# Narrow rows for a second group of modulation weights, softmax scaling on another engine, and a new order of work and loads

## The chip, the cores and the metric

The kernel runs on one core of a Trainium2 chip. The metric is the device time of one execution in microseconds (us), lower is better; the number given for a kernel is the median of its timed runs. The core has five engines that run their own instruction queues in order and wait for each other by semaphores: TensorE (PE; its weight loads are listed apart as PEld), VectorE (DVE), ScalarE (ACT), GpSimd (POOL) and SyncE (SP), which here issues all loads.

## What is computed

Two blocks in float32, batch 1, 256 tokens of width 1024, with a second stream of 256 context tokens in the first of the first block's two layers.

```python
def first_block(x, c, ctx, c_ctx, w_mod, b_mod, ...):
    xl, xc = x, ctx
    for i in range(DEPTH):                      # 2 layers
        ml = (jax.nn.silu(c) @ w_mod[i] + b_mod[i]).reshape(B, N_MOD, 1, D)
        mc = (jax.nn.silu(c_ctx) @ w_mod[i] + b_mod[i]).reshape(N_MOD, D)
        hl = modulate(xl, ml[:, 0], ml[:, 1])
        hc = modulate(xc, mc[0], mc[1])
        if i % 2 == 0:                          # latent attention and pooling windows
            oc, ol = mla_pool_mixer(hc, hl, mix0_w_in[j], ...)
        else:                                   # grouped-query attention
            oc, ol = gqa_mixer(hc, hl, gqa_w_in[j], ...)
        xl = xl + ml[:, 2] * ol
        xl = xl + ml[:, 5] * conv_ffn(modulate(xl, ml[:, 3], ml[:, 4]), ...)
        if not last:
            ...                                 # the same for xc
    return rms_norm(xl, g_final)
```

`modulate(x, shift, scale)` is `rms_norm(x) * (1 + scale) + shift`. The second block is an FFN, a mixer of differential and dilated attention with gates, and another FFN.

## The kernel before, in words

Each weight and activation is split into a high and a low part (`whi`, `wlo`) of the type fp32r, and a product is three matmuls (`mm3`) or two (`mm2`). A weight comes by DMA into one of three `raw` tiles, ACT copies the high part out of it and DVE subtracts it for the low part (`parts`).

Nothing is issued in the order in which the code is written. `Program.record` collects every operation with its dependencies, and `Program.schedule` places them on the five engines by a list schedule: it prices each operation (`price`), adds latencies between engines, gives out tiles from pools (`SLOTS`), and of what is ready takes the one with the lowest index, moved by `shift`. The order in which operations start in this plan is the order on each engine's queue. So a new price or a new rule of the planner moves instructions on every engine.

The parts that matter here, in order of time:

- `setup` loads `cc` (the two conditioning vectors, padded to 32 columns), one stream's X, `ident`, `vecs` and the first pair of `wm` tiles, and issues 100 filler matmuls (`warm`) whose result is not used.
- `mod_chunk(k)` computes shift and scale of layer 0's first normalisation for one of eight blocks of 128 columns. Its 16 matmuls have `sc`, 32 columns wide, as weights, so each uses 32 columns of the array, and four of them stand beside each other. I call a matmul of that shape a narrow row.
- `layer0_mixer` takes the sums of squares (`norm`), and for each of eight k-blocks computes h (`modulated`) and accumulates `p` (pooling input), `cq` of the first stream; then `ckv` of the first stream, transposes (`cT`), the same two products for the second stream, the pooling windows on POOL and DVE (tiles `pp`, `df`, `d`, product `po`), `uk`, `uv`, `uq`, and attention over eight heads (`qkT`, scores `s`, softmax in `e`, transposes `pt`, output `o`).
- `mod_group(g)` computes the other modulation vectors, six groups with eight `raw` tiles each. For a group in `WHOLE` (before: group 0) PE multiplies each tile with four narrow rows. For the others DVE accumulates `raw` times a column of `sc` in `macc`, and PE sums the result over partitions at the end. Group 1 is computed beside `uk` to `uq`, group 0 beside the attention, and groups 2 to 5 beside the FFN of layer 0.
- `softmax_t` has the row maximum on DVE, exp on ACT, the reciprocal on DVE and the scaling (`times`) on DVE for the wide rows of layer 0 (512), on ACT for its narrow ones (256) and for layer 1 (512).

## Time and profile before

| | us |
|---|---|
| three timed runs | 1569.17, 1565.89, 1565.12 |
| their median | 1565.89 |
| the profiled execution | 1562.85 |
| its span, first to last instruction | 1561.1 |
| PE busy | 1534.3 (98%) |
| DVE busy | 1147.6 (74%) |
| ACT busy | 829.1 (53%) |
| POOL busy | 100.1 (6%) |

The share of the longest engine says what bounds the kernel as a whole, but it is an average over stages, and a matmul that is counted as busy may be filler. The rows further down therefore come from stretches of the span. In rows of a timeline the first two numbers are the start in us from the beginning of the span and the busy time of the group of instructions; `xN` is their number, and what stands in brackets is the engine's idle time just before and what ended it. A matmul with fp32 operands (a narrow row, for one) leaves two records; a transpose, or a matmul with fp32r operands, leaves one.

### The profile page before, as it was taken

To read this page: it belongs to the slowest core of one execution; us is meant where nothing else is said; L and a number is where in the kernel's file an instruction comes from. 1 tells how busy PE (TensorE), PEld (TensorE's weight loads), DVE (VectorE), ACT (ScalarE), POOL (GpSimd) and SP (SyncE) were. 2 spreads that over 40 slices of the span, in tenths; PEclk is the share of its full clock that TensorE was granted. 3 is DMA by queue.
4 is the path that set the end of the run, shared out by engine and by line. 5 is a ranking of instruction groups with operands and counts; after the bars stand their busy time and mean duration, and the time that the engine had idled before them with its cause. 6 is when DMAs were issued, how large, how long until landed. Compare 5 with 4: busy or idle time off the path is not lost.

```text
span 1561.1 us, 23690 instructions
## 1 busy us (share of the span) xinstructions
PE 1534.3 (98%) x9226; PEld 1340.2 (86%) x9226; DVE 1147.6 (74%) x2117; ACT 829.1 (53%) x1532; POOL 100.1 (6%) x116
## 2 busy tenths in 40 slices
PE   9989999999999999999999999999999999999998
PEld 7877798888788888999888888888999999888886
DVE  5598889648964856889987787765887786687752
ACT  5356844231331334686876675554765565475550
POOL 0040000000000000110000011100000000111100
PEclk9999999999999999999999999999999999999999
DMA  9345353334753642222665564455423345454450
GB/s 373 117 133 215 135 177 133 123 109 180 257 185 133 245 155 86 84 107 109 237 221 192 177 227 162 163 206 197 166 87 114 122 168 200 173 216 162 162 189 27
DMA packets 41375, 258.47 MB, mean 166 GB/s; under 512 B 4784, under 2 KB 5168, under 8 KB 15664
## 3 DMA queue, kind: packets, MB, share of 16 engines
q1 hardware_dynamic: 41264, 256.97, 45.9%
q8 instruction: 72, 1.18, 0.3%
q14 instruction: 39, 0.32, 0.1%
HBM read 255.90 MB, written 1.05 MB: 165 GB/s over the span
## 4 chain that ended last, share of the span: by engine, by line
PE 88%; DVE 4%; ACT 1%; issue 1%; POOL 1%; DMA 0%; DVEq 0%; POOLq 0%; ACTq 0%; SPq 0%
PE g L401 18%; PE u L401 18%; PE dn L401 12%; PE tm L401 10%; PE y L401 8%; PE out L401 4%; PE gate L401 3%; PE s L401 3%; PE o L401 3%; PE pt L401 2%; PE pa L401 1%; PE mod L401 1%; PE uq L401 1%; DVE wlo L401 1%; DVE h L401 1%
## 5 line engine op out<-in xcount | busy, mean ns | idle before, releaser
L401 DVE TENSOR_TENSOR wlo<-raw,whi 128x1024 fp32r<-128x1024 f32 (+4 forms) x393 | 460.3, 1185 | 81.7 <-PE y L401 26.8
L401 ACT ACTIVATE whi<-raw 128x1024 fp32r<-128x1024 f32 (+4 forms) x393 | 394.1, 1025 | 221.5 <-PE dn L401 59.8
L401 PE MATMUL dn<-mid,whi 128*128 128x512 f32 (+1 forms) x576 | 172.2, 373 | 0.0
L401 PE MATMUL g<-h,whi 128*128 128x512 f32 (+1 forms) x528 | 169.7, 388 | 0.9 <-ACT h L401 0.8
L401 PE MATMUL u<-h,whi 128*128 128x512 f32 (+1 forms) x528 | 167.9, 385 | 0.0
L401 PE MATMUL tm<-whi,a 128*128 128x256 f32 (+1 forms) x576 | 126.8, 306 | 0.1
L401 PEld LDWEIGHTS dn<-mid,whi 128*128 128x128 f32 x576 | 105.0, 188 | 20.4 <-issue 0.8
L401 PE MATMUL dn<-mid,wlo 128*128 128x256 f32 (+1 forms) x376 | 121.6, 323 | 0.0
L401 PE MATMUL g<-a,whi 128*128 128x512 f32 x336 | 118.9, 392 | 0.0
L401 PE MATMUL u<-a,whi 128*128 128x512 f32 x336 | 118.7, 392 | 0.0
L401 PEld LDWEIGHTS g<-h,whi 128*128 128x128 f32 x528 | 99.2, 190 | 22.6 <-ACT h L401 0.9
L401 PEld LDWEIGHTS u<-h,whi 128*128 128x128 f32 x528 | 98.8, 188 | 19.8
L401 PE MATMUL g<-h,wlo 128*128 128x256 f32 (+1 forms) x344 | 115.0, 335 | 0.4 <-DVE wlo L401 0.4
L401 PE MATMUL u<-h,wlo 128*128 128x256 f32 (+1 forms) x344 | 114.6, 333 | 0.0
L401 PE MATMUL y<-whi,mid 128*128 128x512 f32 x352 | 109.0, 389 | 0.0
L401 DVE SCALAR_TENSOR_TENSOR macc<-raw,sc,macc 128x1024 f32<-128x1024 f32 x84 | 107.0, 1298 | 2.6 <-DMA raw<-wmod 2.4
L401 PEld LDWEIGHTS tm<-whi,a 128*128 128x128 f32 x576 | 95.2, 190 | 1.4 <-DVE a L401 0.3
L401 PE MATMUL g<-a,wlo 128*128 128x256 f32 x336 | 94.2, 280 | 0.0
L401 PE MATMUL u<-a,wlo 128*128 128x256 f32 x336 | 94.1, 280 | 0.0
L401 POOL TENSOR_TENSOR small<-small,mhalf 128x2 f32<-128x2 f32 (+2 forms) x34 | 34.2, 1007 | 895.1 <-DVE small L401 725.3
L401 PE MATMUL tm<-wlo,a 128*128 128x256 f32 (+1 forms) x288 | 87.6, 305 | 0.0
L401 PEld LDWEIGHTS y<-whi,mid 128*128 128x128 f32 x352 | 66.1, 188 | 13.7
(342 smaller groups left out, 3205.4 us busy)
## 6 DMA issues: line engine op xcount, KB each, us to landing
raw<-wup SPq DMA_DIRECT2D x44, 1024.0 KB, 4.8
raw<-wgu SPq DMA_DIRECT2D x44, 1024.0 KB, 4.8
raw<-wmod SPq DMA_DIRECT2D x32, 1024.0 KB, 5.0
raw<-wd SPq DMA_DIRECT2D x20, 1024.0 KB, 4.7
raw<-wdn SPq DMA_DIRECT2D x16, 1024.0 KB, 4.8
raw<-win2a SPq DMA_DIRECT2D x12, 1024.0 KB, 4.8
raw<-win2d SPq DMA_DIRECT2D x12, 768.0 KB, 4.2
wm<-wmod SPq DMA_DIRECT2D x16, 512.0 KB, 10.6
```

Source lines behind the costliest of these rows:

```text
L401: getattr(getattr(nc, op.engine), op.method)(*[res(a) for a in op.args], **{k: res(v) for k, v in op.kw.items()})
```

## The change

The host packs `cc` without padding, and the 32-column `sc` is cleared on DVE and filled by a small activation. Both streams' X are loaded first, then the first `wm` pair, then `ident` and `vecs`. The filler falls from 100 to 50 matmuls. The sums of squares are taken 512 wide, half of the pieces on ACT and half on DVE. Group 1 joins group 0 in `WHOLE`. The first `macc` instructions of group 2 get an additional dependency on the end of the FFN's first normalisation (`late`). All softmax scalings of layers 0 and 1 go to POOL. In the planner, a row of narrow matmuls is kept in one piece (`together`), the two edges of such a run and the read port that DVE and POOL both use are modelled, a PSUM tile counts as one region, at most eight loads are under way, and several prices are new.

```diff
-WHOLE = (0,)
+WHOLE = (0, 1)
...
+    ENTER, LEAVE = 90.0, 230.0
...
-    DMA_RATE = 330.0
+    DMA_RATE = 400.0
+    DMA_BEGIN = 2000.0
+    DMA_DEPTH = 8
...
+    def together(self, i):
+        group = self.ops[i:]
+        for op in group[1:]:
+            group[0].deps |= {d for d in op.deps if d < i}
+        for a, b in zip(group, group[1:]):
+            a.next = b
...
     def region(v):
+        if v.root.cls == "psum":
+            return (0, P, 0, v.root.ix.size)
...
             if op.kw["lhsT"].root.dtype == F32R:
-                return n / 2.4 * (1 if n >= 256 else 4) + 2.5
-            c = max(128, n) * 4 / 2.4 + 2.5
-            return c * 0.25 + 15 if width == 32 else c
+                return n / 2.4 + 13.3
+            return 0.4 * n if out.parts[1] - out.parts[0] == 32 else 222.0
...
+    def shared(op):
+        big = [v for v in list(op.args) + list(op.kw.values()) if isinstance(v, View)
+               and v.root.cls != "psum" and not any(v is o for o in op.outs)]
+        if op.engine == "gpsimd":
+            return len(big) > 0
+        if op.engine != "vector":
+            return False
+        big = [v for v in big if v.ix.size > 1]
+        return len(big) > 1 or (op.method in ("tensor_copy", "tensor_scalar") and len(big) == 1
+                                and op.outs[0].root.cls != "psum")
...
+            if self.shared(op):
+                other = "gpsimd" if e == "vector" else "vector"
+                t = max(t, port[other])
+                port[e] = t + cost
...
-        cc = self.tmp(KD * 32, "cc").rearrange("p (k n) -> p k n", k=KD)
+        cc = self.small(16).rearrange("p (k n) -> p k n", k=KD)
         nc.sync.dma_start(out=cc, in_=ap["cc"])
         self.sc = self.const([P, KD, 32], "sc")
-        nc.scalar.activation(self.sc, cc, AF.Silu)
+        nc.vector.memset(self.sc, 0.0)
+        nc.scalar.activation(self.sc[:, :, 0:2], cc, AF.Silu)
...
-        for _ in range(100):
+        for _ in range(50):
             nc.tensor.matmul(ps[:, :T], lhsT=warm[:, :P], rhs=warm, start=True, stop=True)
...
-        for c in range(0, KD, 4):
-            nc.sync.dma_start(out=self.X[0][:, c:c + 4], in_=ap["xc"][0, :, c:c + 4])
+        for s in range(2):
+            for c in range(0, KD, 4):
+                nc.sync.dma_start(out=self.X[s][:, c:c + 4], in_=ap["xc"][s, :, c:c + 4])
+        self.wm = {}
+        self.load_mod(0)
         nc.sync.dma_start(out=self.ident, in_=ap["ident"])
         nc.sync.dma_start(out=self.vecs, in_=ap["vecs"])
-        self.wm = {}
-        self.load_mod(0)
...
             if g in WHOLE:
                 ps = ps or self.ps("mod")
+                first = len(nc.ops)
                 for q in range(4):
                     nc.tensor.matmul(ps[32 * q:32 * q + 32, :w], lhsT=self.sc[:, k, :], rhs=r[:, q * w:(q + 1) * w],
                                      start=(k == 0), stop=(k == KD - 1))
+                nc.together(first)
...
                             nc.vector.tensor_scalar(acc[h, s], x, c, None, op0=ALU.mult)
+                            if g == 2:
+                                nc.ops[-1].deps.add(self.late)
...
         def norm(s):
-            acc = self.acc(s)
-            for k in range(KD):
-                self.sq_add(acc, self.xs(k, s), k == 0)
-            rb.append(self.norm_rows(acc))
+            part = []
+            for k0 in range(0, KD, 4):
+                sq = self.actf("sq")
+                for o in (0, 2):
+                    x = self.X[s][:, k0 + o:k0 + o + 2].rearrange("p k n -> p (k n)")
+                    if o:
+                        nc.vector.tensor_tensor(sq[:, 512:], x, x, op=ALU.mult)
+                    else:
+                        nc.scalar.activation(sq[:, :512], x, AF.Square)
+                nc.vector.tensor_tensor(sq[:, :512], sq[:, :512], sq[:, 512:], op=ALU.add)
+                part.append(sq[:, :512])
+            nc.vector.tensor_tensor(part[0], part[0], part[1], op=ALU.add)
...
-                    es.append(self.softmax_t(pscore[:, :nk * P], nk * P, "scalar" if s else "vector"))
+                    es.append(self.softmax_t(pscore[:, :nk * P], nk * P, "gpsimd"))
...
+        self.late = len(self.nc.ops) - 1
...
-                    es.append(self.softmax_t(pscore, 512, "scalar"))
+                    es.append(self.softmax_t(pscore, 512, "gpsimd"))
```

What this does to the queues shows at three places. The first is PE's queue at the start. Before, filler stands between the first `cq` matmuls and the second stream's sums, and single narrow rows (`mod` from `wm`) stand among other matmuls:

```order
L401 MATMUL cq_316<-whi_280,h_302 128x384
L401 MATMUL cq_322<-whi_280,h_302 128x384
L401 MATMUL warm_131<-warm_101 128x256 x26
L401 MATMUL sum_379<-ones,acc_309 128x1 x2
L401 MATMUL mod_382<-wm_112,sc 32x128
L401 MATMUL warm_131<-warm_101 128x256 x2
L401 MATMUL ckv_386<-whi_280,h_302 128x288
```

The same place now; the rows end where the second chunk's sixteen narrow rows begin:

```order
L459 MATMUL rows_239<-ident,small_202 128x128 x2
L459 MATMUL mod_208<-sel,modsb_237 128x4
L459 MATMUL sum_245<-ones,sq_164 128x1 x4
L459 MATMUL rows_274<-ident,small_268 128x128 x2
L459 MATMUL cq_279<-whi_255,h_272 128x384
L459 MATMUL cq_279<-wlo_262,h_272 128x384
L459 MATMUL cq_286<-whi_255,h_272 128x384
L459 MATMUL cq_286<-wlo_262,h_272 128x384
L459 MATMUL mod_292<-wm_161,sc 32x128
```

The second stream's sums moved ahead of the first `cq`, the filler left this place (all 50 now stand ahead of the first `mod`), and each chunk's narrow rows follow one another.

The second place is DVE's queue ahead of the second stream's `cqraw` copies, from which PE's second set of `cT` transposes is made. Before:

```order
L401 TENSOR_SCALAR macc_1054<-raw_785,sc 128x1024
L401 SCALAR_TENSOR_TENSOR df_1060<-pp_183_1025,pp_110 128x512
L401 TENSOR_TENSOR wlo_1067<-raw_594,whi_1040 128x1024
L401 TENSOR_TENSOR d_1072<-df_1060,d_1072 128x512
L401 TENSOR_SCALAR macc_1090<-raw_785,sc 128x1024
L401 SCALAR_TENSOR_TENSOR macc_1054<-raw_1019,sc,macc_1054 128x1024
L401 SCALAR_TENSOR_TENSOR macc_1090<-raw_1019,sc,macc_1090 128x1024
L401 COPY cqraw_1126<-cq_942 128x384
L401 COPY cqraw_1126<-ckv_963 128x288
```

And now:

```order
L459 SCALAR_TENSOR_TENSOR df_940<-pp_167_909,pp_86 128x512
L459 TENSOR_TENSOR wlo_948<-raw_576,whi_921 128x1024
L459 TENSOR_TENSOR d_951<-df_940,d_951 128x512
L459 TENSOR_TENSOR wlo_989<-raw_576,whi_972 128x1024
L459 TENSOR_TENSOR pp_171_999<-pp_171_999,consts 128x2
L459 COPY cqraw_1026<-cq_860 128x384
L459 TENSOR_SCALAR small_1037<-small_1021 128x1
L459 COPY cqraw_1026<-ckv_879 128x288
```

The four `macc` instructions are gone from ahead of the copies, and the two `wlo` splits and one `d` stay.

The third place is PE's queue in the attention of layer 0, where group 0's narrow rows (`mod` from `raw`) stand. Before, in one of several such places:

```order
L401 MATMUL o_1733<-pT_1814,v_1300 64x256
L401 MATMUL pt_1832<-ident,e_1790 128x128
L401 MATMUL mod_1533<-raw_1591,sc 32x512
L401 MATMUL pt_1836<-ident,e_1790 128x128
L401 MATMUL mod_1533<-raw_1591,sc 32x512
L401 MATMUL s_1842<-qkT_1367,qkT_1692 128x256 x3
```

And now:

```order
L459 MATMUL pt_1698<-ident,e_1648 128x128
L459 MATMUL pt_1698<-ident,e_1659 128x128
L459 MATMUL s_1712<-qkT_1556,qkT_1549 128x512 x3
L459 MATMUL mod_1450<-raw_1496,sc 32x512 x4
L459 MATMUL o_1737<-pT_1700,v_1115 64x256 x3
L459 MATMUL o_1737<-pT_1700,v_1151 64x256 x3
```

The four rows of one tile now follow one another. Over the attention the 32 narrow rows stand in 15 runs before and in 8 after.

## Rows read from the trace of the kernel before

**Rows 1.** Busy us of the engines over the whole span; mean of 22 stretches

```profile
sum 1561.00, PE 1534.34 PEld 1340.16 DVE 1147.56 ACT 829.15 POOL 100.14; mean PE 69.74 PEld 60.92 DVE 52.16 ACT 37.69 POOL 4.55
```

**Rows 2.** Stretches: busy us (count) of PE, PEld, DVE, ACT, POOL; clock, DMA, GB/s

```profile
0.00:40.00 40.00, 36.26 (x342) 30.88 (x343) 23.78 (x61) 20.08 (x44) 3.82 (x11) 1.00 0.97 374
...
64.40:71.25 6.85, 6.85 (x53) 6.85 (x52) 1.61 (x5) 1.76 (x6) 0.00 (x0) 1.00 0.21 77
...
93.75:128.00 34.25, 33.89 (x185) 28.78 (x185) 33.16 (x68) 21.07 (x41) 4.70 (x11) 0.95 0.46 152
128.00:185.40 57.40, 57.38 (x378) 40.27 (x377) 46.24 (x109) 42.81 (x106) 0.00 (x0) 1.00 0.46 169
...
251.00:600.00 349.00, 349.00 (x1609) 286.62 (x1608) 238.13 (x312) 115.29 (x159) 0.00 (x0) 1.00 0.47 169
```

**Rows 3.** Timeline of all engines from the beginning to 26 us

```profile
9.25 0.38 PE L401 MATMUL mod<-wm,sc 128*32 128x128 f32 x2 [1.19 <-DMA wm<-wmod]
...
17.16 3.28 PE L401 MATMUL warm<-warm 128*128 128x256 f32 x26
...
25.12 1.16 PE L401 MATMUL p<-h,whi 128*128 128x512 f32 x2 [0.39 <-ACT h L401]
```

**Rows 4.** Timeline of PE, where matmuls of 512 and 384 follow each other

```profile
407.90 0.62 PE L401 MATMUL u<-h,whi 128*128 128x512 f32 x2
408.35 0.39 PE L401 MATMUL u<-h,wlo 128*128 128x512 f32 x1
...
73.61 0.52 PE L401 MATMUL cq<-whi,h 128*128 128x384 f32 x2
73.97 0.34 PE L401 MATMUL cq<-wlo,h 128*128 128x384 f32 x1
```

**Rows 5.** Timeline of PE, 71 to 94 us

```profile
71.25 1.03 PE L401 MATMUL cT<-ident,cqraw 128*128 128x128 f32 x8
...
88.58 0.40 PE L401 MATMUL po<-d,wlo 128*128 128x512 f32 x1
93.75 1.33 PE L401 MATMUL cT<-ident,cqraw 128*128 128x128 f32 x5 [4.77 <-DVE cqraw L401]
```

**Rows 6.** Timeline of DVE, 82 to 94 us

```profile
82.90 1.58 DVE L401 TENSOR_SCALAR macc<-raw,sc 128x1024 f32<-128x1024 f32 x1
...
89.12 4.11 DVE L401 SCALAR_TENSOR_TENSOR macc<-raw,sc,macc 128x1024 f32<-128x1024 f32 x2
93.15 0.55 DVE L401 COPY cqraw<-cq 128x384 f32<-128x384 f32 x1
```

**Rows 7.** Timeline of PE, runs of narrow rows

```profile
131.86 1.06 PE L401 MATMUL mod<-raw,sc 128*32 128x512 f32 x8
...
149.67 1.04 PE L401 MATMUL mod<-raw,sc 128*32 128x512 f32 x2
...
124.98 0.64 PE L401 MATMUL mod<-macc,one 128*32 128x256 f32 x8
...
46.57 1.07 PE L401 MATMUL mod<-wm,sc 128*32 128x128 f32 x30
```

**Rows 8.** POOL's groups by shape: count, busy us, mean ns; idle before

```profile
L401 POOL TENSOR_TENSOR pp<-pp 128x542 f32<-128x542 f32 x4 | 5.7, 1434 | 3.1 <-PE ckv L401 1.8 <-DVE df L401 1.3
...
L401 POOL MEMSET pp<- 128x544 f32 x4 | 2.2, 588 | 0.0
```

**Rows 9.** DVE's groups by shape

```profile
L401 DVE TENSOR_TENSOR wlo<-raw,whi 128x1024 fp32r<-128x1024 f32 x348 | 421.7, 1224 | 77.4 <-PE y L401 26.8 <-PE dn L401 18.2 <-ACT whi L401 12.9
...
L401 DVE TENSOR_SCALAR e<-e,small 128x512 f32<-128x512 f32 x16 | 7.7, 479 | 0.2
...
L401 DVE TENSOR_TENSOR d<-df,d 128x512 fp32r<-128x512 f32 x4 | 4.6, 1158 | 0.4 <-ACT d L401 0.3
```

**Rows 10.** ACT's groups by shape

```profile
L401 ACT ACTIVATE e<-e,small 128x512 f32<-128x512 f32 x16 | 10.8, 727 | 0.0
...
L401 ACT ACTIVATE e<-e,small 128x256 f32<-128x256 f32 x16 | 7.8, 510 | 0.1
```

More of the change, by code (lines that the diff above doesn't have):

```diff
@@ L274, in price, with load @@
             if op.kw.get("op") == ALU.pow:
-                return 300 + 165.0 * n
+                return 700.0
             return 100 + n * {"tensor_tensor": 2.3, "tensor_scalar": 1.46, "memset": 0.8}.get(m, 3.5)
         return 60.0
+    @staticmethod
+    def load(op):
+        if op.method != "transpose" and op.outs[0].parts[1] - op.outs[0].parts[0] == 32:
+            return 0.0
+        return 109.0
+    @staticmethod
+    def shared(op):
[8 more added lines that the diff above has]
+                                and op.outs[0].root.cls != "psum")
     def nbytes(self, op):
@@ L304, in schedule @@
         clock = {e: 0.0 for e in self.ENGINES}
-        dma, heat, table = 0.0, {}, None
+        dma, heat, table = self.DMA_BEGIN, {}, None
+        port = {"vector": 0.0, "gpsimd": 0.0}
+        begun, narrow, follow = 0.0, False, None
+        landed = []
         done = np.zeros(N + 1, bool)
@@ L314, in schedule @@
             for e in self.ENGINES:
-                if avail[e]:
+                if e == "tensor" and follow is not None:
+                    t = clock[e]
+                elif avail[e]:
                     t = clock[e]
@@ L328, in schedule @@
                 heapq.heappush(avail[e], (p, i))
-            _, i = heapq.heappop(avail[e])
+            if e == "tensor" and follow is not None:
+                i = follow.index
+                avail[e].remove((follow.prio, i))
+                heapq.heapify(avail[e])
+            else:
+                _, i = heapq.heappop(avail[e])
             op = ops[i]
@@ L350, in schedule @@
                 live[r.cls][front:r.first] += 1
+            cost = op.cost
+            if self.shared(op):
+                other = "gpsimd" if e == "vector" else "vector"
+                t = max(t, port[other])
+                port[e] = t + cost
+            if e == "tensor":
+                load = self.load(op)
+                t = max(t, begun + load)
+                if narrow != (load == 0.0):
+                    t = max(t, clock[e] + (self.LEAVE if narrow else self.ENTER))
+                begun, narrow = t, load == 0.0
+                follow = op.next
             op.start = t
-            cost = op.cost
             if e == "tensor":
@@ L363, in schedule @@
             if e == "sync":
+                landed.append(op)
+                if len(landed) > self.DMA_DEPTH:
+                    t = max(t, landed[-1 - self.DMA_DEPTH].end)
+                    op.start, clock[e] = t, t + cost
                 begin = max(t, dma)
@@ L656, in mod_group @@
                                      start=(k == 0), stop=(k == KD - 1))
+                nc.together(first)
             else:
@@ L669, in mod_group @@
         ps = ps or self.ps("mod")
+        first = len(nc.ops)
         for s in range(streams if acc else 0):
@@ L674, in mod_group @@
                                  start=(s == 0), stop=(s == streams - 1))
+        if acc:
+            nc.together(first)
         sb = self.tmp(w, "modsb")
@@ L786, in norm @@
         def norm(s):
-            acc = self.acc(s)
-            for k in range(KD):
-                self.sq_add(acc, self.xs(k, s), k == 0)
-            rb.append(self.norm_rows(acc))
-        norm(0)
+            part = []
[5 more added lines that the diff above has]
+                        nc.vector.tensor_tensor(sq[:, 512:], x, x, op=ALU.mult)
+                    else:
+                        nc.scalar.activation(sq[:, :512], x, AF.Square)
+                nc.vector.tensor_tensor(sq[:, :512], sq[:, :512], sq[:, 512:], op=ALU.add)
+                part.append(sq[:, :512])
+            nc.vector.tensor_tensor(part[0], part[0], part[1], op=ALU.add)
+            total = self.ps("sum")
+            for j in range(2):
+                for k in range(2):
+                    o = k * T + j * P
+                    nc.tensor.matmul(total[:, j:j + 1], lhsT=part[0][:, o:o + P], rhs=self.ones[:, 0:1],
+                                     start=(k == 0), stop=(k == 1))
+            r = self.row("rb")
+            nc.scalar.activation(r, self.rows(self.rsqrt(total[:, 0:2], 1.0 / D, EPS, 2)), AF.Copy)
+            rb.append(r)
+        for s in range(2):
+            norm(s)
         wa, wp = {}, {}
```

24 lines of the change are left out of this document (9 added, 15 removed).

## The prediction

> **What bounds the kernel now.** I read the page's first block, then the table of stretches, then the timelines of the stretches in which TensorE (PE) is not simply streaming. PE is busy 1534.3 us of 1561.1, and in the long stretch from 251 to 600 us it is busy in all 349.00 us [rows 1, 2]. Nothing that another engine does can shorten that stretch, and the diff removes no matmul there. So only the places count where PE waits, runs filler, or runs work that costs more than its columns. There are four, all in the first 190 us.
>
> First, the start. Filler matmuls (`warm`) stand in PE's queue until 20 us: 26 of them run from 17.16 to 20.4. The first `p` matmul starts at 25.12, and the first transpose `cT` not before 71.25 [rows 3, 5]. DMA moves 374 GB/s over the first 40 us [rows 2], so loads set when the work can begin.
>
> Second, the wait at 88.6. PE has issued a `po` matmul at 88.58 and then waits 4.77 us for `cqraw` [rows 5]. On VectorE (DVE), four `macc` instructions lie between 82.9 us and that copy; the last two take 4.11 us, to 93.2 [rows 6]. After the wait the granted clock averages 0.95 over 34.25 us: PE ran for part of it at the lower of its two levels, 1.2 GHz instead of 2.4, which is 1.7 us lost (0.05 of 34.25) [rows 2].
>
> Third, the narrow rows (32 columns of the array) of group 0 in the attention. Four of them in one run (x8 in the trace, two records each) are busy for 1.06 us, a single one (x2) for 1.04 [rows 7]. A run has one price whatever it holds, up to four.
>
> Fourth, the softmax of layer 0's attention, where PE is busy in 57.38 of 57.40 us, DVE in 46.24 and ScalarE (ACT) in 42.81 [rows 2]: PE decides, but the others have little room.
>
> **The change part by part.** The sum is made against the profiled execution: 1562.85 us, of which 1561.1 is the span. The median of the three timed runs is 1565.89, 3.04 above it, and I carry that difference over unchanged.
>
> *Start.* Both streams are now loaded ahead of the first weights, half of the filler is gone, and the squares are taken in 512-wide pieces on two engines. PE's new queue has each chunk of 16 narrow rows in one run, and puts chunk 7 ahead of the last part of `p` and `cq`. Up to and including chunk 7's weights the new load queue holds 8 + 2048 + 64 + 157 + 8192 + 2688 + 2048 = 15205 KB (c, both X, ident, vecs, 16 `wm`, four `win0a`, four `win0p`, from their shapes), 15.57 MB, or 41.6 us at 374 GB/s. Before the change, the first `mod` waited for its 512 KB until 9.25 [rows 3] with 1885 KB queued up to it, 5.2 us at that rate, so a landing comes about 4.1 us later than the quotient. That puts chunk 7 at 45.7. Behind it PE has: the chunk, 1.25 (1.07 for 15 of 16 rows [rows 7], and the way in); six `p` matmuls at 0.227 and six `cq` at 0.18 [rows 4], 2.4; three more k-blocks of twelve and six, 11.4; and the 48 `ckv`, 6.85 by the stretch that holds almost only these [rows 2]. Together 21.9, so `cT` at 67.6: 3.7 us earlier than 71.25. This counts the slow beginning of the loads twice, once in the rate and once in the 4.1; counted once, the gain is 7.8. I take 6, nearer to the middle. Against it, PE now waits for loads between short bursts from about 9 to 22 us with nothing to fill them. The row after the 4.77 us wait shows what follows on such a wait, so I put in one clock drop, 1.7 us. Start: -4.3, between +3 (no gain, two drops) and -8. The small c load takes 120 KB from the queue, 0.3 us, inside that range; the 0.3 us `sc` work is off the path.
>
> *Group 1 on PE.* `WHOLE = (0, 1)` takes 16 `macc` instructions from DVE, the four of the second place among them; group 2's are held back until the FFN's first normalisation, so nothing of that kind is left on DVE before the attention ends. The 4.77 us and the 1.7 us go. What is late next is the copy chain itself: two `cqraw` copies of 0.55 [rows 6], so I leave 1.2 us of wait. Second place: -5.3, between -2 (the chain of the pooling windows on GpSimd (POOL), which runs in the same stretch, keeps half the wait) and -6.5. PE pays for it: eight runs of four narrow rows, 256 wide. The nearest row is a run of the same shape, 0.64 busy [rows 7]; with the way in and out 0.72. Eight of them are 5.8, less the two such runs that summed `macc` before, 1.4: +4.3 (3 to 6).
>
> *Runs kept together.* In PE's order the 32 narrow rows of group 0 stand in 15 runs before and in 8 after. Seven runs less at 1.05: -7.4. PE is full in this stretch, so all of it should show if the others keep up; -4 if half is handed back as waits.
>
> *Softmax scaling on POOL.* 48 instructions move, 16 of them 512 wide from DVE (479 ns), 16 of 512 and 16 of 256 from ACT (727 and 510 ns) [rows 9, 10]. The trace has no one-input arithmetic on POOL. Below lies the 544-wide memset, 588 ns, which reads nothing; above the 542-wide addition, 1434 ns, with two inputs and DVE in its way [rows 8]. For 512 that is 0.55 to 1.35; I take 0.8, nearer to the memset, since one input is missing from the addition. Each of the 24 softmaxes has two such scalings in a row on POOL. At 0.8 the eight wide ones of layer 0 grow by 2 x (0.8 - 0.479) = 0.64 each, its eight narrow ones shrink by 0.2, those of layer 1 grow by 0.15: +4.8 if PE waited for all of it. The next head's matmuls cover part, and DVE and ACT lose 7.7 and 20 us of work: +2. At 0.55 it is -5, at 1.35 up to +27.
>
> The Trainium skill speaks against this edit: "SBUF — State Buffer", section "Who interferes with whom", says that a VectorE instruction with both inputs in SBUF and a GpSimd instruction that reads SBUF exclude each other for their whole length. The trace agrees: the four `d` subtractions, 512 wide with both inputs in SBUF and issued among POOL's additions, average 1158 ns, hardly less than a `wlo` split of 1024 with 1224 [rows 9]. By the rule, a scaling that meets a `wlo` split waits for it.
>
> *Everything else.* The planner's new prices change the order of layer 1's attention and of the last block's mixer, not of the FFNs. PE's whole idle time is 26.8 us [rows 1], and outside the places above little of it is left: 0, plus or minus 3.
>
> Sum: -4.3 - 5.3 + 4.3 - 7.4 + 2 = -10.7. The profiled execution would take 1552.2 us, the median 1555.2.
>
> **The rivals.**
> - *POOL becomes the bound of the attention.* The scaling costs 1.35 and stands between exp and the transposes, so that PE waits. Without the softmax term the sum is -12.7; the change ends slower than before by over 0.3% (4.7 us) once that term passes 17.4 us, two thirds of the 27. At 20 us: 1573.2. For it speaks the 1434 ns row, against it that PE's new order holds other heads' matmuls between. The rule of the skill above would act in this direction.
> - *The start gives nothing.* Loads arrive as late as by the slow reckoning, and the clock falls more than once between the bursts. Start +3 in place of -4.3: -3.4, 1562.5. For it: the filler that bridged these waits is halved. The Trainium skill, "TensorE: Matmul & The Clock Gate", section "HAM oscillation — how this bites in real kernels", describes bursts shorter than the loads between them, each of which starts again at the lower clock.
> - *The wait at 88.6 stays* and only changes its releaser, to the pooling chain on POOL: the 5.3 us do not come, -5.4, 1560.5. This is the case in which the change does not do what it says.
> - *All of it lands:* start -8, scaling at 0.55 hidden, so -1 for the lighter DVE and ACT: with -8, -1, -5.3, +4.3 and -7.4 about -17.4, 1548.5.
>
> **How the numbers follow.** A measurement of this kernel tells about 0.3%, 4.7 us, from no change. Forecast 1555 (1550 to 1560): 0.64. All of it lands: 0.12. Start gives nothing: 0.12. The wait stays: 0.05. POOL bound: 0.07. Faster by over 0.3% means under 1561.2: 0.63 + 0.12 + 0.03 + 0.04 = 0.82. Within: 0.01 + 0.08 + 0.01 + 0.02 = 0.12. Slower: 0.06, nearly all of it POOL. The range 1547 to 1563 takes in the forecast and the cases beside it, and leaves out the POOL case and the outer parts of the others.
>
> **What would show it.** The first `cT` at 64 to 68 us and not 71. No PE wait over 1.5 us for `cqraw`, and a granted clock of 1.00 after it. Eight runs of x8 `mod<-raw,sc` at 512 and eight at 256, the latter 0.6 to 0.8 each. POOL's scaling of 512 near 0.8 us, and no `pt` wait on POOL that adds up to over 4 us. The stretch 251 to 600 with the same length, only earlier. I would be wrong if a lower clock shows between 9 and 25 us for more than a few us, if the `pt` transposes become PE's main wait, or if layer 1's attention grows by more than 3 us.

## The result and the profile after

The changed kernel takes 1576.55 us (median of four runs, 1574.96 to 1577.8); the kernel before takes 1565.56 on the same terms (1565.12 to 1569.17). The ratio is 1.0067, with a 95% interval from 1.0050 to 1.0084. The forecast was 1555.2, with a range from 1547 to 1563. The kernel became 11 us slower where I had said 10.7 us faster.

The profiled execution of the changed kernel took 1576.12 us, its span 1574.3. First the page's block of busy times, then the table of stretches (PE, PEld, DVE, ACT, POOL, then clock, DMA share, GB/s), which answer [rows 1] and the last line of [rows 2]:

```profile
PE 1536.3 (98%) x9232; PEld 1336.0 (85%) x9232; DVE 1126.9 (72%) x2082; ACT 814.8 (52%) x1488; POOL 171.8 (11%) x164
```

```profile
9.00:25.00 16.00, 13.12 (x161) 10.99 (x161) 11.28 (x29) 7.50 (x15) 2.29 (x2) 1.00 1.03 409
...
246.60:595.60 349.00, 348.06 (x1602) 285.62 (x1601) 248.27 (x316) 118.57 (x162) 0.00 (x0) 1.00 0.51 182
```

PE's busy time has hardly moved (1534.3 to 1536.3) while the span grew by 13.2 us, so PE waits more. DVE and ACT lost work (1147.6 to 1126.9, 829.1 to 814.8), and POOL has 71.7 us more. The long FFN stretch is nearly as full as before (348.06 of 349.00 us; before, all of them), and the clock in the start is 1.00.

The start and the second place, in PE's timeline (answers [rows 5] and a line of [rows 7]). The first two lines are of the kernel before, the first `uk` and the first attention product `s`; the others are of the changed kernel:

```profile
97.17 0.40 PE L401 MATMUL uk<-whi,ckvT 128*128 128x512 f32 x1
...
129.12 0.50 PE L401 MATMUL s<-qkT,qkT 96*128 96x512 f32 x1
```

```profile
66.49 0.92 PE L459 MATMUL cT<-ident,cqraw 128*128 128x128 f32 x7
...
82.41 0.39 PE L459 MATMUL po<-d,whi 128*128 128x512 f32 x1
82.64 0.70 PE L459 MATMUL cT<-ident,cqraw 128*128 128x128 f32 x4
83.57 0.33 PE L459 MATMUL cT<-ident,cqraw 128*128 128x128 f32 x1 [0.24 <-ACT junk L459]
...
84.53 0.40 PE L459 MATMUL uk<-whi,ckvT 128*128 128x512 f32 x1
...
87.62 0.64 PE L459 MATMUL mod<-raw,sc 128*32 128x256 f32 x8
...
119.81 0.47 PE L459 MATMUL s<-qkT,qkT 96*128 96x512 f32 x1
```

The first `cT` is at 66.49 and no longer at 71.25. The wait of 4.77 us for `cqraw` is gone; 0.24 is left. `uk` begins at 84.5 and no longer at 97.2, and the first `s` 9.3 us earlier than before (119.8, 129.1). Up to there the change does what it should.

Then the waits of PE in the attention of layer 0 (120 to 235 us) and of layer 1 (612 to 725 us), in the view of waits (sum, times, longest), each the largest row of its stretch:

```profile
PE pt L459 <- POOL e L459: 8.2, 12, 1.5
...
PE pt L459 <- POOL e L459: 5.8, 9, 1.3
```

No such row existed before. POOL's groups by shape show the price (answers [rows 8], where the trace had no scaling):

```profile
L459 POOL TENSOR_SCALAR e<-e,small 128x512 f32<-128x512 f32 x32 | 55.5, 1744 | 69.2 <-DVE small L459 60.1 <-PE s L459 8.3 <-ACT e L459 0.7
...
L459 POOL TENSOR_SCALAR e<-e,small 128x256 f32<-128x256 f32 x16 | 16.6, 1048 | 6.3 <-DVE small L459 6.3
...
L459 POOL TENSOR_TENSOR pp<-pp 128x542 f32<-128x542 f32 x4 | 4.4, 1094 | 4.2 <-PE ckv L459 2.6 <-DVE df L459 1.6
```

A scaling of 512 takes 1744 ns on average, where ACT took 727 and DVE 479 [rows 9, 10]. One place in layer 1 shows what that does. The timelines of POOL, DVE and PE there:

```profile
688.62 2.75 POOL L459 TENSOR_SCALAR e<-e,small 128x512 f32<-128x512 f32 x1
```

```profile
688.54 1.22 DVE L459 TENSOR_TENSOR wlo<-raw,whi 128x1024 fp32r<-128x1024 f32 x1
```

```profile
688.70 0.44 PE L459 MATMUL pt<-ident,e 128*128 128x128 f32 x2 [0.27 <-POOL e L459]
...
689.67 0.40 PE L459 MATMUL out<-att,whi 128*128 128x512 f32 x1
691.42 0.76 PE L459 MATMUL pt<-ident,e 128*128 128x128 f32 x5 [1.35 <-POOL e L459]
```

The transposes `pt` of one head need two scaled tiles. The second scaling begins at 688.62, just behind the start of a `wlo` split on DVE, and ends at 691.37. PE has put five `out` products between, then runs dry and waits 1.35 us.

Where the 11 us come from is best read by cutting each trace at three places: the first FFN product of layer 0 (`g<-h`), the first product of layer 1 (`tm<-whi,h`), and the first FFN product of layer 1 (`g<-xd`). The FFN between the first two takes 374.3 to 376.4 us in every kernel of this study, so three numbers are left. All are worked out from the starts of matmuls (the last column ends with the last matmul); "before again" is a second trace of the unchanged kernel (experiment 8), which lies nearer to that kernel's median than the first.

| kernel | time, median | ratio to before, 95% | `g<-h` begins | layer-1 attention | `g<-xd` to the end |
|---|---|---|---|---|---|
| before | 1565.56 | 1 | 242.6 | 102.0 | 834.5 |
| before again (8) | 1567.29, one run | | 243.6 | 103.4 | 836.4 |
| changed | 1576.55 | 1.0067 [1.0050, 1.0084] | 238.2 | 112.5 | 842.7 |
| scaling back on ACT and DVE (1) | 1560.91 | 0.9956 [0.9939, 0.9973] | 231.3 | 106.9 | 837.5 |
| before, scaling on POOL (2) | 1585.82 | 1.0115 [1.0088, 1.0143] | 252.8 | 113.6 | 837.9 |
| changed, true price in the planner (3) | 1565.92 | 0.9988 [0.9977, 0.9999] | 230.5 | 110.0 | 842.5 |
| before, new start (4) | 1567.12 | 1.0003 [0.9989, 1.0017] | 241.6 | 103.9 | 837.4 |
| (1) without group 1 (5) | 1575.15 | 1.0054 [1.0037, 1.0071] | 241.8 | 107.1 | 842.1 |
| (1) with runs not held (6) | 1563.65 | 0.9989 [0.9975, 1.0004] | 234.4 | 106.6 | 843.2 |
| (3) with layer 1 scaled on ACT (7) | 1560.87 | 0.9968 [0.9956, 0.9981] | 230.3 | 107.0 | 838.6 |
| (1) without any scaling (9) | 1559.56 | 0.9949 [0.9933, 0.9965] | 228.8 | 103.9 | 839.2 |
| before, group 1 on PE (10) | 1570.20 | 1.0027 [1.0014, 1.0041] | 246.4 | 103.5 | 840.5 |
| before, new start and group 1 (11) | 1567.65 | 1.0010 [0.9996, 1.0024] | 242.4 | 103.6 | 837.4 |
| before, new planner alone (12) | 1574.80 | 1.0044 [1.0027, 1.0060] | 244.5 | 106.7 | 839.4 |

Against "before again" the changed kernel is 5.4 us ahead at `g<-h`, loses 9.1 us in layer 1's attention, 6.3 behind it, and gains 0.7 in the FFN between.

### The profile page after: what moved, and what is told of

It reads as the page before. It is cut to its first block, busy times and chain, and to the rows that moved or that the text cites. A ratio compares the mean times of both kernels' runs of the same rounds, so it can differ in the third digit from the quotient of the medians.

```text
span 1574.3 us, 23777 instructions
## 1 busy us (share of the span) xinstructions
PE 1536.3 (98%) x9232; PEld 1336.0 (85%) x9232; DVE 1126.9 (72%) x2082; ACT 814.8 (52%) x1488; POOL 171.8 (11%) x164
## 3 DMA queue, kind: packets, MB, share of 16 engines
HBM read 255.78 MB, written 1.05 MB: 163 GB/s over the span
## 4 chain that ended last, share of the span: by engine, by line
PE 65%; DVE 6%; ACT 2%; DMA 2%; issue 1%; POOL 1%; DVEq 0%; POOLq 0%; ACTq 0%; SPq 0%
PE u L459 15%; PE g L459 15%; PE dn L459 9%; PE tm L459 8%; PE y L459 8%; PE gate L459 3%; PE pa L459 1%; DVE small L459 1%; DVE macc L459 1%; DVE wlo L459 1%; PE o L459 1%; PE s L459 1%; PE pt L459 1%; ACT whi L459 1%; POOL e L459 1%
## 5 line engine op out<-in xcount | busy, mean ns | idle before, releaser
L459 DVE SCALAR_TENSOR_TENSOR macc<-raw,sc,macc 128x1024 f32<-128x1024 f32 x70 | 87.7, 1282 | 8.3 <-DMA raw<-wmod 8.3
L459 POOL TENSOR_SCALAR e<-e,small 128x512 f32<-128x512 f32 (+1 forms) x48 | 71.8, 1512 | 75.6 <-DVE small L459 66.5
## 6 DMA issues: line engine op xcount, KB each, us to landing
wm<-wmod SPq DMA_DIRECT2D x16, 512.0 KB, 10.6
```

The costliest lines, as they stand in the source:

```text
L459: getattr(getattr(nc, op.engine), op.method)(*[res(a) for a in op.args], **{k: res(v) for k, v in op.kw.items()})
```

## The experiments

The theory was that the scaling on POOL stands on the path from `s` to `pt` and PE waits for it. The rival was that the new plan as a whole, its prices and its order, is the loss. Experiments 1 and 2 take this from both sides, 3 and 7 ask why the scaling is that dear, 9 what there was to gain. Experiments 4, 5, 6, 10, 11 and 12 take the remaining parts alone and together, and 8 asks what belongs to a single execution. Each comparison is with runs of the kernel before on the same chip.

**1. The scaling back, everything else changed.**

```diff
-    es.append(self.softmax_t(pscore[:, :nk * P], nk * P, "gpsimd"))
+    es.append(self.softmax_t(pscore[:, :nk * P], nk * P, "scalar" if s else "vector"))
...
-    es.append(self.softmax_t(pscore, 512, "gpsimd"))
+    es.append(self.softmax_t(pscore, 512, "scalar"))
```

> The changed kernel with one part undone: the softmax scaling of the two attentions goes back to ScalarE and VectorE, everything else (start, group 1 on TensorE, kept-together runs, prices) stays changed. Theory A (the scaling on GpSimd is the loss): attention of layer 0 gets back the 5 us and attention of layer 1 the 8 to 10 us that it lost, the waits of TensorE in front of pt<-ident,e fall from 5.8 us to under 1 us in layer 1, and the time is 1559 to 1564 us, below the kernel before. Theory B (the new plan as a whole, its prices and its order, is the loss): the waits in front of the transposes go, but other waits take their place and the time is 1572 us or more. Beside that the steady products g<-a with a moving operand of two runs show a period of 230 ns if their slower period in the changed kernel (237 ns) hangs on the attention, and 237 ns if it does not.

Measured: 1560.91 us, ratio 0.9956. PE's largest waits in layer 1's attention (606 to 713 us):

```profile
PE tm L459 <- ACT h L459: 1.1, 2, 0.8
PE pt L459 <- ACT e L459: 0.9, 1, 0.9
```

Theory A holds: with the scaling back the change is a gain. Between the two ratios lie 0.0111, or 17.4 us of 1566 (15.6 between the medians): this is what the softmax term cost. It came out of all three columns of the table (6.9, 5.6 and 5.2 us). The first two parts, 12.5 us, hold the two attentions, where PE waited 14.0 us for POOL; layer 1's gave back less than the 8 to 10 us that theory A had. The last part holds no scaling, and is taken up under experiment 8.

**2. The scaling on POOL alone, on the kernel before.**

```diff
-            self.nc.vector.tensor_scalar(x, x, r, None, op0=ALU.mult)
+            getattr(self.nc, engine).tensor_scalar(x, x, r, None, op0=ALU.mult)
...
-    es.append(self.softmax_t(pscore[:, :nk * P], nk * P, "scalar" if s else "vector"))
+    es.append(self.softmax_t(pscore[:, :nk * P], nk * P, "gpsimd"))
...
-    es.append(self.softmax_t(pscore, 512, "scalar"))
+    es.append(self.softmax_t(pscore, 512, "gpsimd"))
```

> The kernel before with one part done alone: the softmax scaling of both attentions on GpSimd, the planner's old prices and nothing else. Theory A: some 15 us slower than the kernel before, 1577 to 1583 us, TensorE waits in front of pt<-ident,e in both attentions. Theory B: within 3 us of the kernel before, 1563 to 1569 us.

Measured: 1585.82 us, ratio 1.0115, so 18 us slower, a little more than expected. PE's largest wait over the whole span, and then the worst place, in the timelines of POOL, DVE and PE:

```profile
PE pt L401 <- POOL e L401: 12.8, 19, 3.7
```

```profile
196.48 5.32 POOL L401 TENSOR_SCALAR e<-e,small 128x512 f32<-128x512 f32 x1 [6.77 <-DVE small L401]
```

```profile
196.71 1.21 DVE L401 TENSOR_TENSOR wlo<-raw,whi 128x1024 fp32r<-128x1024 f32 x1
...
197.91 1.20 DVE L401 TENSOR_TENSOR wlo<-raw,whi 128x1024 fp32r<-128x1024 f32 x1
...
199.17 1.20 DVE L401 TENSOR_TENSOR wlo<-raw,whi 128x1024 fp32r<-128x1024 f32 x1
```

```profile
197.53 0.61 PE L401 MATMUL out<-att,whi 128*128 128x512 f32 x2
201.86 0.69 PE L401 MATMUL pt<-ident,e 128*128 128x128 f32 x2 [3.72 <-POOL e L401]
```

The cost is there without any other part of the change. One scaling lasts 5.32 us, and three `wlo` splits run on DVE in its time: from the end of the third, 200.37, to its own end at 201.80 are 1.43 us, a little less than a scaling takes by itself. PE stands for 3.72 us behind it.

**3. The true price in the planner.**

```diff
-            return 100 + n * {"tensor_tensor": 2.3, "tensor_scalar": 1.46, "memset": 0.8}.get(m, 3.5)
+            if m == "tensor_scalar":
+                return 350 + 2.72 * n
+            return 100 + n * {"tensor_tensor": 2.3, "memset": 0.8}.get(m, 3.5)
```

> The changed kernel with one number changed: the planner's price of a GpSimd scaling is the measured one (1744 ns at 512 wide and 1048 ns at 256 wide, in place of 848 and 474). Theory A1 (the planner puts the transposes too early because it takes the scaling for half as long): with the true price it fills the time with other matmuls, the 5.8 us in front of pt<-ident,e in layer 1 shrink below 2 us, and the time is 1565 to 1570 us. Theory A2 (there is nothing left to fill with, the longer chain itself is the loss): the waits stay and the time is 1574 to 1579 us.

Measured: 1565.92 us, ratio 0.9988. POOL's group and PE's largest wait in layer 1's attention (606 to 716 us); in layer 0's attention no wait on POOL is left in the view:

```profile
L461 POOL TENSOR_SCALAR e<-e,small 128x512 f32<-128x512 f32 x32 | 52.3, 1643 | 69.7 <-DVE small L461 66.6 <-PE qkT L461 3.1
```

```profile
PE pt L461 <- POOL e L461: 1.8, 3, 1.1
```

Theory A1 holds. One price in the planner's table gives back 10.6 of the 15.6 us between the medians, and layer 0 is then as fast with the scaling on POOL (`g<-h` at 230.5) as with it on ACT and DVE (231.3). The scaling itself is hardly shorter: of the 48, 7 are lengthened by a split where 11 were. But PE's waits for it fall from 14.0 to 1.8 us in the views, since the planner puts other matmuls in between. Layer 1 keeps a loss, 110.0 us against 106.9; that there is less to put in between there is an argument and was not tried.

**4. The new start alone, on the kernel before.** The edit is the parts of the diff in `setup` (small `cc`, 50 fillers, both X first), in `norm` and in the load order of `layer0_mixer`.

> The kernel before with one part done alone: both streams loaded first, squares 512 wide on two engines, the small load of c, 50 warm-up products in place of 100. If the 4.7 us that the changed kernel was ahead at the first cT transpose reach the end: 1560 to 1562 us. If they are lost in the second place (the wait for cqraw before cT) or at the entry of layer 1: 1564 to 1567 us.

Measured: 1567.12 us, ratio 1.0003: no gain. The first `cT` comes at 68.15, 3.1 us earlier than before. In PE's timeline the second set of `cT` still waits for `cqraw`, and begins 3.1 us earlier than at 93.75:

```profile
90.64 1.33 PE L401 MATMUL cT<-ident,cqraw 128*128 128x128 f32 x5 [4.77 <-DVE cqraw L401]
```

The 3 us are still there at this point, 2.0 at `g<-h` against "before again", and 0.9 at the end, within what one execution differs from another.

**5. Group 1 back on DVE.**

```diff
-WHOLE = (0, 1)
+WHOLE = (0,)
```

> The version with the scaling back on ScalarE and VectorE (e1_scale_back, 1560.9 us), and group 1 of the modulation back on VectorE's running sums. By the prediction's terms: TensorE gets back the 4.3 us of group 1's narrow products (24 products more and their runs), but the second place loses what the sums cost it: the 4.8 us wait for cqraw in front of cT returns, and uk begins some 5 us later, so the time is within 2 us of e1_scale_back: 1559 to 1563 us. Rival: the new order and the earlier second stream cover that wait without group 1; then it is 1556 to 1558 us. Other rival: the sums hold VectorE up in the attention too, 1564 us or more.

Measured: 1575.15 us, 14 us slower than (1) (15 by the ratios). Of the three expectations only the last, which was open upwards, takes it in. DVE's costliest group between 67 and 135 us, PE's waits from 60 to 240 us, and the stretch from 105 to 135 us:

```profile
L459 DVE SCALAR_TENSOR_TENSOR macc<-raw,sc,macc 128x1024 f32<-128x1024 f32 x14 | 17.5, 1280 | 0.0
```

```profile
PE uq L459 <- ACT whi L459: 2.5, 1, 2.5
PE uq L459 <- DVE wlo L459: 2.0, 1, 2.0
PE po L459 <- DVE pool L459: 1.9, 1, 1.9
PE qkT L459 <- DVE v L459: 1.7, 2, 1.0
```

```profile
105.00:135.00 30.00, 22.41 (x107) 18.86 (x108) 27.30 (x45) 8.65 (x16) 0.00 (x0) 0.72 0.65 225
```

The `cqraw` wait does not return. The new plan puts the sums later, among the splits of `uq`'s weights, which PE then waits for; it runs dry several times, and the granted clock averages 0.72 over 30 us. The first `s` comes at 134.9, 15 us later than in (1).

**6. Runs not held together.**

```diff
     def together(self, i):
+        return
         group = self.ops[i:]
```

> The version with the scaling back on ScalarE and VectorE, and the narrow products no longer held together: the planner may put other products between them (the program then has 38 runs of narrow products where e1_scale_back has 28). By the prediction's term (1.05 us for each run more): 10 runs more, 10.5 us, 1569 to 1574 us. Rival: a planner that has the price of entering and leaving a narrow run in its table breaks a run only where TensorE would wait anyway; then it is within 3 us, 1558 to 1564 us.

Measured: 1563.65 us, 2.7 us above (1), as the rival had it; by the ratios 5.2. The ten runs more cost a quarter to a half of the 10.5 us that 1.05 for each would make. The first `cT`, in (1) and here, shows that the start needs them held:

```profile
66.55 1.03 PE L459 MATMUL cT<-ident,cqraw 128*128 128x128 f32 x8
```

```profile
71.04 1.03 PE L460 MATMUL cT<-ident,cqraw 128*128 128x128 f32 x8
```

Counted in PE's order, seven of the ten runs more stand in the start (15 runs of `wm` rows, 8 in (1)) and three behind it. From the first `s` to `g<-h` this kernel takes 110.0 us and (1) 111.4. So what (6) loses up to `g<-h`, 3.1 us, it loses in the start, and the experiment does not measure what the runs held together in the attention are worth.

**7. POOL for layer 0 alone, with the true price.** On the kernel of (3):

```diff
-    es.append(self.softmax_t(pscore, 512, "gpsimd"))
+    es.append(self.softmax_t(pscore, 512, "scalar"))
```

> The scaling on GpSimd in layer 0 alone, with its measured price in the planner's table; in layer 1 on ScalarE as before. Theory: in layer 0 there is other work to put behind a scaling once its price is true (narrow products, the pools), in layer 1 there is not. Then the end of the layer-0 mixer (the lam product) is at 227 to 229 us as in e3_true_price and e1_scale_back, the layer-1 attention takes 105 to 107 us, not 110, and the time is 1557 to 1561 us. Rival: layer 0 pays for the GpSimd scaling too; lam comes after 230 us and the time is 1563 us or more.

Measured: 1560.87 us, ratio 0.9968; `g<-h` at 230.3, layer 1's attention 107.0 us. As expected: in layer 0 POOL may have the scaling if the price is right, but nothing is gained by it over (1).

**8. The kernel before again.**

> The kernel before once more, nothing changed. What is looked at is the period of the two-run products in the four stretches 775 to 900, 950 to 1025, 1275 to 1325 and 1400 to 1475 us, which was 231.6, 230.0, 235.9 and 230.0 ns in the first trace, and the granted clock in the first 8 us of layer 1, which was 1.00. If period and clock belong to the program, they come out the same to 0.2 ns and 0.01. If they belong to the single execution, at least one of the stretches comes out at another level (230, 231.6, 236 or 236.7 ns) and the clock at 0.7 to 0.85.

Measured: 1567.29 us. The first lines are of the first trace, the second of this one (stretches: first of layer 1, then 75 us of the last FFN):

```profile
617.60:625.60 8.00, 8.00 (x67) 8.00 (x68) 6.75 (x19) 3.92 (x11) 0.70 (x1) 1.00 0.00 0
...
1400.00:1475.00 75.00, 75.00 (x435) 66.14 (x434) 52.26 (x90) 42.55 (x78) 10.37 (x14) 1.00 0.47 163
```

```profile
618.60:626.60 8.00, 8.00 (x55) 8.00 (x56) 5.46 (x15) 3.04 (x7) 0.69 (x1) 0.80 0.00 0
...
1400.00:1475.00 75.00, 75.00 (x426) 65.06 (x425) 51.80 (x91) 42.11 (x78) 9.56 (x13) 1.00 0.44 160
```

The same program, but in the first 8 us of layer 1 the clock fell to 0.80 (12 matmuls fewer), and in the last FFN 426 matmuls run in the time of 435. Many products here (`mm2`) are pairs of matmuls, the first with a moving operand of 512 columns in two runs of 256, the second with 256 columns. From one pair to the next PE takes 346.7 ns in one execution and 353.4 in the other (means over the 189 and 186 pairs of that stretch), with PE busy throughout. I call that the period. The kernel has 1360 such pairs, so about 9 us lie between all at one level and all at the other. So a part of the last column of the table belongs to the execution. Not all of it need: in the FFN of layer 1, all six traces with the old plan show the short period, those with the new plan and no POOL scaling in layer 1 too except for (9), and the changed kernel and (3) the long one. The stretch from 775 to 900 us, of the changed kernel and of (1):

```profile
775.00:900.00 125.00, 125.00 (x710) 108.56 (x709) 97.75 (x160) 82.63 (x140) 0.00 (x0) 1.00 0.55 195
```

```profile
775.00:900.00 125.00, 125.00 (x723) 110.20 (x723) 95.52 (x154) 78.76 (x134) 0.00 (x0) 1.00 0.53 189
```

Summed over the pairs that a trace holds behind `g<-xd` (some 1140), the longer period makes 4.7 of the 5.2 us that lie between the changed kernel and (1) in the last column. What sets the level there was not tried, so whether these 5.2 us belong to the scaling stays open; the 12.5 in the attentions do. In (1) itself the period is short from 775 to 900 us and long from 950 to 1025 (353.4), so the question that its expectation asks of the period has no single answer.

**9. No scaling at all.**

```diff
         nc.vector.reciprocal(r, l)
-        self.times(engine, e, r)
         return e
```

> The version with the scaling back on ScalarE and VectorE (e1_scale_back, 1560.9 us), but the scaling of the softmax numerators is left out altogether: the kernel doesn't divide by the sums, so part of the computation is missing. It measures what the scaling costs where it was. If the scaling on ScalarE and VectorE was hidden already, there was nothing to gain by moving it: within 3 us of e1_scale_back, 1558 to 1564 us. If it stood on TensorE's path, its 727 ns on ScalarE come off the chain of each of the later softmaxes and the time falls by 5 us or more, to 1556 us or less.

Measured: 1559.56 us, 1.3 us below (1), and their intervals overlap. Its trace shows more: `g<-h` begins 2.5 us earlier and layer 1's attention is 3.0 us shorter, but 1.7 of that is the clock in the first 8 us of layer 1, 1.00 here and 0.79 in (1), which belongs to the execution (8). So on ACT and DVE the scaling cost some 1 to 4 us in this plan. It is no exact bound on what moving it can gain: leaving it out changes the plan too, and the first `cT` comes 1.4 us later here than in (1).

**10. Group 1 on PE alone, and 11. with the new start, both on the kernel before.**

```diff
-WHOLE = (0,)
+WHOLE = (0, 1)
```

> The kernel before with one constant changed: group 1 of the modulation on TensorE as narrow products, the old prices, the old start, nothing held together. By the prediction's terms (second place 5.3 us less, group 1 4.3 us more): 1565 us, no difference. By what leaving group 1 out cost in e5_no_group1 (14 us): if that was VectorE's time alone, this one gains 5 us or more even with the old start, 1556 to 1561 us; if it was group 1 and the early start together, this one is at 1563 to 1568 us and e11_start_group1 is the one that gains.

> The kernel before with the new start and with group 1 on TensorE, the old prices and nothing held together. By the prediction's terms (4.3 and 5.3 us less, 4.3 us more): 1560 to 1562 us. If the start can only pay once VectorE is free of group 1's sums: 1557 to 1562 us here against 1567 us for the start alone (e4_start_only). If the new prices and the held runs are what carries the gain of e1_scale_back: 1565 to 1568 us.

Measured: 1570.20 (ratio 1.0027) and 1567.65 (1.0010). Group 1 alone costs 4 us: the wait for `cqraw` is gone from the view, but the narrow rows now stand in 43 runs, not 36 (counted in PE's order), and `g<-h` begins 2.8 us later than in "before again". With the new start the two cancel. 1570 lies above all three expectations of 10, and what its third goes on to say, that (11) is the one that gains, does not come true. The prices and the held runs are needed too, as the last line of 11 says.

**12. The new planner alone.** The edit is the `Program` class of the changed kernel, `together` and `late` with their calls; start, `WHOLE` and scaling stay as before.

> The kernel before with the new planner alone: the new prices, narrow runs held together, the sums of groups 2 and later held back; the old start, group 1 on VectorE, the scaling on ScalarE and VectorE. By the prediction's terms (7.4 us for the runs, nothing for the rest): 1557 to 1561 us. By e6_not_held (holding worth some 3 us) and e5_no_group1 (the new plan with group 1's sums on VectorE lost 9 us even with the new start): no gain, 1565 to 1577 us.

Measured: 1574.80 us, ratio 1.0044, 6.9 us slower. As in (5), 14 `macc` stand in DVE's row between 66 and 137 us. Layer 1's attention takes 106.7 us, not 103.4, though nothing in it is changed but the order: a loss of the plan, which (1), (5), (6) and (7) show too (106.6 to 107.1). The first `cT` comes at 68.27: the planner alone, too, brings 3 us of the start's gain.

## Why the prediction was wrong, and where it was right

*Start, -4.3.* Right in place, and in size by luck: first `cT` 4.76 us earlier, said 64 to 68, came at 66.5. But I had taken a gain of 6 and put in one clock drop of 1.7 us between the bursts; the clock from 9 to 25 us is 1.00 and none came, so the two errors cancel. The gain needs the held runs as well: without them the first `cT` is at 71.04 (6), as before. The Trainium skill describes in "TensorE: Matmul & The Clock Gate", section "HAM oscillation — how this bites in real kernels", that bursts between loads each begin again at the lower clock. The trace doesn't show that here, though the filler was halved and PE was busy for only 13.12 of those 16 us.

*Second place, -5.3.* Right, and too small: no `cqraw` wait over 0.24 us, clock 1.00, and the lead grew from 4.8 us at `cT` to 12.6 at `uk`. A part of that is order: some `cT` and `po` stood ahead of `uk` before and stand behind it now.

*Group 1, +4.3.* About right as a price: the lead shrank from 12.6 to 9.3 between `uk` and `s`, and a run shows 0.64 busy as taken. But the term was a price on one engine and not a worth. Left out of the otherwise new kernel, group 1 makes it 14 us slower (5); put alone into the old one, 4 us slower (10).

*Runs kept together, -7.4.* Too large as far as the runs show. From the first `s` to `g<-h` the kernel before takes 113.5 us and (1) 111.4, so 2.1 of the 7.4 arrive. PE is given time back as waits, the case I had put at -4: before, it was idle for 0.02 us of this stretch up to 185.4 [rows 2], and in (1) it is idle for 2.48 us of 53, and the clock averages 0.97.

```profile
120.00:173.00 53.00, 50.52 (x367) 40.29 (x367) 46.08 (x101) 45.17 (x105) 0.00 (x0) 0.97 0.55 199
```

What held runs are shown to be worth by (6), 4.5 us at the first `cT`, is in the start, where the prediction had no term of their own for them.

*Softmax scaling, +2 (-5 to +27).* This is the step that failed. It measures 17.4 us as the difference of two ratios (1), 12.5 of them in the two attentions. I had taken 0.8 us for a scaling of 512, "nearer to the memset, since one input is missing from the addition", with 1.35 as the upper end. It takes 1.56 when nothing is in its way (the median of 32), and 1.74 on average: above the end that I had called the upper one, and longer than the two-input addition of 542, 1094 ns in this trace, that I had set it below. A row of another operation was no bound. The second half of the step, that the next head's matmuls cover part, holds only if the planner knows the price; it had 847 ns. With the true one, 10.6 us come back (3). (The parts of the forecast at 0.8 add up to 4.7, not 4.8, which changes nothing.)

The rule of the Trainium skill ("SBUF — State Buffer", section "Who interferes with whom") is that a VectorE instruction with both inputs in SBUF and a GpSimd instruction that reads SBUF contend for a shared port pair, with an exclusive lock. The trace agrees with it in part. Of 48 scalings in the changed kernel, 11 take longer than 1.65 us (512) or 1.0 (256), and each of these 11 has a `wlo` split, with both its inputs in SBUF, running at its start (one split begins 0.02 us behind it). The 2.75 us at 688.62 are one split of 1.22, begun 0.08 earlier, and 1.6 of its own; the 5.32 us of (2) span three splits. But the prediction had read it as exclusion for their whole length, and the measurement differs: a scaling holds a split up for only a part of its own length. The first pair of lines is of the changed kernel, the second of (3):

```profile
657.31 1.56 POOL L459 TENSOR_SCALAR e<-e,small 128x512 f32<-128x512 f32 x1
657.93 1.21 DVE L459 TENSOR_TENSOR wlo<-raw,whi 128x1024 fp32r<-128x1024 f32 x1
```

```profile
178.93 1.57 POOL L461 TENSOR_SCALAR e<-e,small 128x512 f32<-128x512 f32 x1 [0.54 <-DVE small L461]
179.07 1.62 DVE L461 TENSOR_TENSOR wlo<-raw,whi 128x1024 fp32r<-128x1024 f32 x1
```

A split that begins 0.62 us into a scaling runs beside it for 0.94 us, and neither is longer. One that begins 0.14 us into it takes 1.62 instead of 1.21, and the scaling is not longer. By these numbers a scaling of 512 holds a split up only until some 0.55 us after its own start (0.14 + 1.62 - 1.21, an estimate). So what lengthens a scaling is a split that runs when it starts, or begins just behind that. Which of two near starts goes first is not settled: in (2) the first split begins 0.23 us into the scaling, and it is the scaling that waits. This explains the difference between 1.56 and 1.74 and the longest waits. It doesn't explain the 1.56.

*Everything else, 0 plus or minus 3.* A little outside its margin: the new plan makes layer 1's attention 3.3 us longer by itself (12, against "before again", one trace each). Which of its prices does that was not tried.

*The sum.* Without the softmax term I had -12.7; (1) measured -6.9 by its ratio, and in the profile -12.3 at `g<-h`, of which layer 1's attention takes back 3.5. So the terms up to layer 1 add up, but by luck: (1) is 10.3 us ahead of "before again" at the first `s`, where the terms had 5.3, and gains 2.0 from there to `g<-h`, where they had 7.4. And adding them was wrong as a method. By the ratios start alone, group 1 alone and planner alone are +0.5, +4.2 and +6.9 us, together 11.6 us slower; all three at once are 6.9 us faster. As far as their traces show, each had its loss in what the others repaired: the earlier data ran into DVE's sums, group 1 on PE stood in too many runs, and the new plan piled the sums up in front of `uq`.

*The rivals.* "POOL becomes the bound of the attention" is what happened, by its own mechanism: PE waits for the scaling between exp and transposes, 14.0 us in the two attentions. It gave 1573.2, and its point of decision, a softmax term of 17.4 us, is just what was reached, by chance, since 5.2 of it stand behind the attentions; with the other terms short of their forecast, the time is 1576.55. I gave it 0.07, because I trusted that PE's order held other heads' matmuls between. The other three did not come by their mechanisms, though the start alone is worth nothing at the end (4). My own list of signs told it all: a scaling near 0.8, `pt` waits on POOL under 4 us, and layer 1's attention growing by no more than 3 us all failed; the signs of start, second place and FFN came true.

The version with the scaling back (1) beats both kernels: 0.9956 of the time before, about 7 us.

## What to carry to other kernels

Price an operation on an engine that has never run it by measuring it, and put that number into the planner's table before moving anything there: a scheduler that believes 847 ns for 1744 puts the consumer too early, and correcting that one price gave back 10.6 of 15.6 us. Before moving an operation off a path, leave it out once: some 1 to 4 us was all that it cost here. And parts of a change that share an engine's free time cannot be costed one by one: three parts that lose 0.5 (within the noise), 4.2 and 6.9 us alone gain 6.9 together.

## What the runs showed of the hardware

- A multiplication of 128x512 by one scalar per partition on POOL takes 1.56 us, of 128x256 0.92 (medians of 32 and 16); an addition of two tiles of 542 takes 1.09.
- A scaling on POOL that starts while a `wlo` split runs on DVE becomes longer by nearly what is left of the split: 2.75 us with one, 5.32 with three in a row. A split that begins 0.62 us into a scaling changes neither (1.56 and 1.21 at 657 us); one that begins 0.14 us into it becomes longer itself (1.62 at 179 us of (3)).
- PE can stream the same pairs of products with period 346.7 or 353.4 ns, at a granted clock of 1.00 and never idle, and keep to one for 100 us and more. Two executions of one program differ in that over one stretch of 75 us. All pairs at one level or the other would be about 9 us apart in this kernel, more than the whole gain of (1). One trace of each kernel would not have shown it.
- After the two short waits at the entry of layer 1 (1.1 and 0.8 us) the granted clock fell in one execution of the kernel before (0.80 over 8 us) and not in the other (1.00).
